# A later landing time for every transfer in the order finder of a two-layer trunk kernel

## The chip, the cores and the metric

The kernel runs on one core of one Trainium2 chip. The metric is device time in microseconds (us) of one execution. A core has five engines that run side by side, each through its own list of instructions in order: PE (TensorE, matmuls), DVE (VectorE), ACT (ScalarE), POOL (GpSimd) and SP (SyncE, which here only issues DMA transfers). An instruction that must wait for another engine or for a transfer holds up everything behind it in its own list.

## The reference

A trunk of two layers on 256 tokens of width 1024, all in float32. Each layer is a gated feed-forward (width 2816), a mixer with two kinds of attention, and a second gated feed-forward; each of the three is wrapped in a normalization whose shift, scale and gate come from a vector `c`:

```python
for l in range(2):
    mod = silu(c) @ ada_w[l] + ada_b[l]          # 1024 x 9216 weights, one row
    sh1, sc1, g1, sh2, sc2, g2, sh3, sc3, g3 = split(mod, 9)
    h = rmsnorm(x, norm_pre[l, 0]) * (1 + sc1) + sh1
    y = (silu(h @ w_gate) * (h @ w_up)) @ w_down
    x = x + 0.5 * g1 * rmsnorm(y, norm_post[l, 0])
    h = rmsnorm(x, norm_pre[l, 1]) * (1 + sc2) + sh2
    y = mixer(h)                                  # 8 sliding-window heads, 8 causal heads
    x = x + g2 * rmsnorm(y, norm_post[l, 1])
    ...                                           # second feed-forward, with sh3, sc3, g3
```

## The kernel before, in words

**Weights.** Every weight block is 1 MiB. SP loads it into a tile `raw` (pool of 3, `NRAW`), and `unit` splits it by quarters into two halves of the precision: ACT writes `hi` (L450), DVE writes `lo` = raw - hi (L451). A `raw` tile is free for the next load when DVE has written the last quarter of its `lo`. PE multiplies three products per block: in the feed-forward's columns L498 and L501 (`mm2t`, 512 and 256 columns), elsewhere L489, L490 and L491 (`mm3`). The feed-forward runs over the hidden width in 11 blocks of 256 columns, `w_gate` and `w_up` by columns (L498, L501; ACT and DVE empty their PSUM tiles `w` in L725 and L726), `w_down` by rows (accumulators `a`).

**Modulation in the background.** The vectors sh, sc, g that are needed later come from `ada_w`, 512 KiB at a time: SP loads a tile `araw` (L534, pool of 2), DVE multiplies and adds it into `acc` in two instructions (L526, "sums" below), and when eight are done ACT and DVE split the sum (L541, L542) and PE adds it up over the partitions (L543, L544, `over_partitions`), after which ACT or DVE (L554, L557, L560) makes the row. A new `araw` can be issued when the sums of the one two before it are done.

**The opening.** The first two vectors (shift and scale of the first normalization) can't wait for that. They are computed by quarters q of 256 columns on PE itself from tiles `eraw` (L937; L1009 for q = 0, L1013 after), then DVE adds the bias row (L1017), PE spreads the row over the partitions (L1018), DVE applies it to both halves of the tokens (L1026, L1027), and `to_T` turns the result (PE L618) into `hT` (ACT L621, DVE L622). As each quarter is ready, PE multiplies it with a quarter of the first weight columns ("first", four accumulators) and of the next ones ("next", L1047 to L1049).

**The order.** The program is written once, and then `keep_order` decides in which order each engine runs its instructions. It knows an estimated duration of each (`cost`) and plays the program forward: an engine takes, among the instructions that it believes ready, the one of the best priority. A transfer ends in its model when a single queue has moved its bytes, and whoever reads it is ready a fixed time later, `READY["SP"]` for ACT, with values of their own for DVE and PE. `forward` runs once from the written priorities and four times (`FBI`) from those that `backward` derives; the shortest result in its own estimate gives the lists, which are then fixed by order edges between neighbours:

```python
gap = AFTER[e] if eng[j] == e and not dma[k] else READY.get((e, eng[j]), READY[e])
ready[j] = max(ready[j], end + gap if preds[j][k] else start)
```

The hardware then obeys the lists: what the finder believed of the times has no further effect than the order.

Of the kernel before, what the change touches and what calls it, by code (L numbers as in the profile page):

```python
# [41 lines left out]

READY = {("SP", "DVE"): 1000, ("SP", "PE"): 1100, "SP": 910, ("PE", "DVE"): 290, "PE": 200, ("DVE", "PE"): 235,
         "DVE": 200, ("Activation", "PE"): 275, "Activation": 145, "Pool": 60}
AFTER = {"SP": 0, "PE": 0, "DVE": 125, "Activation": 100, "Pool": 90}
FBI, BSLACK, FSLACK = 4, {'DVE': 60, 'Activation': 40}, {'DVE': 370, 'Activation': 810}
# [34 lines left out]
def keep_order(tc, nc, slots, shifts):  # L83
# [72 lines left out]
    def forward(prio):  # L156
# [33 lines left out]
        for _ in range(10 * N):  # L190
# [50 lines left out]
            for j in succs[k]:  # L241
                npred[j] -= 1
                gap = AFTER[e] if eng[j] == e and not dma[k] else READY.get((e, eng[j]), READY[e])
                ready[j] = max(ready[j], end + gap if preds[j][k] else start)
# [9 lines left out]
    def backward(at_, reuse):  # L254
# [16 lines left out]
        while True:  # L271
# [8 lines left out]
            for j, kind in ps[k].items():  # L280
                nsucc[j] -= 1
                if kind is True:
                    gap = AFTER[eng[j]] if eng[j] == e and not dma[j] else READY.get((eng[j], e), READY[eng[j]])
                else:
# [830 lines left out]
```

## Time and profile before

| | |
|---|---|
| median of 3 runs | 1038.66 us (1036.26 to 1040.55) |
| profiled execution | 1039.74 us, its span 1038.0 us |
| PE busy | 1004.7 us, 97% of the span |
| DVE busy | 846.6 us, 82% |
| ACT busy | 597.9 us, 58% |
| mean DMA rate | 252 GB/s |

PE is busy nearly throughout, and 33.3 us of its span are idle. So the time can change only where PE waits: by waits that go, or by new ones. The profiled execution lies 1.74 us above its span, which is what lies around the first and last instruction.

### The profile page before, as it was taken

The page shows a single profiled execution, that of the slowest core. Times are in us where ns is not written, and L with a number is a line of the kernel's source. Part 1 is how long each engine was busy: PE and PEld are TensorE (multiplying, and loading weights), DVE is VectorE, ACT ScalarE, POOL GpSimd, SP SyncE. Part 2 cuts the span into 40 slices and gives each one's busy share as a digit, 9 for nine tenths or more (in the row PEclk, how much of TensorE's full clock was granted, in tenths as well). Part 3 has the DMA queues.
Part 4 walks back from the last instruction along what each step waited for, and adds up shares of the span by engine and source line. Part 5 has one row for each costly group of instructions (what it writes and reads, how often), then busy time and mean ns, then how long its engine had stood idle before and what let it go on. Part 6 is the DMA issues. An engine that isn't in the chain of part 4 may idle for free. (4 is left out here: it accounts for less than half of the span.)

```text
span 1038.0 us, 15309 instructions
## 1 busy us (share of the span) xinstructions
PE 1004.7 (97%) x5386; PEld 840.7 (81%) x5386; DVE 846.6 (82%) x1640; ACT 597.9 (58%) x1398; POOL 44.7 (4%) x92
## 2 busy tenths in 40 slices
PE   7999998999999999999999999999999999999997
PEld 4787877788887888888888888888788778888886
DVE  3698998888996898898989988988978789665652
ACT  3365545564676875656756655554577766554541
POOL 1000000001001100000010000000200020000000
PEclk9999999999999999999999999999999999999999
DMA  9999889785997388788757988887589638555521
GB/s 322 340 332 333 271 295 313 261 288 191 315 316 259 94 286 296 239 289 296 255 202 263 308 290 286 316 278 280 174 285 329 207 123 290 182 197 187 182 78 40
DMA packets 171976, 261.82 MB, mean 252 GB/s; under 512 B 6524, under 2 KB 107612, under 8 KB 171900
## 3 DMA queue, kind: packets, MB, share of 16 engines
q1 hardware_dynamic: 171744, 260.78, 74.5%
q8 instruction: 42, 0.69, 0.3%
q14 instruction: 34, 0.28, 0.1%
q10 hardware_dynamic: 156, 0.07, 0.0%
HBM read 259.76 MB, written 1.07 MB: 251 GB/s over the span
## 5 line engine op out<-in xcount | busy, mean ns | idle before, releaser
L451 DVE TENSOR_TENSOR lo_a<-raw_a,hi_a 128x512 fp32r<-128x512 f32 (+1 forms) x548 | 296.3, 586 | 25.9 <-PE w_b L501 8.0
L450 ACT ACTIVATE hi_a<-raw_a 128x512 fp32r<-128x512 f32 (+1 forms) x548 | 262.2, 542 | 78.4 <-DMA raw_a<-in_ffn_w_up_dram 18.7
L498 PE MATMUL w_a<-hT,hi_a 128*128 128x512 f32 x608 | 213.2, 398 | 2.7 <-DVE row_b L557 1.3
L498 PE MATMUL w_b<-hT,hi_b 128*128 128x512 f32 x512 | 180.4, 398 | 2.6 <-DVE st_a L726 1.6
L501 PE MATMUL w_a<-hT,lo_a 128*128 128x256 f32 x608 | 158.5, 281 | 0.0
L450 ACT ACTIVATE hi_b<-raw_b 128x512 fp32r<-128x512 f32 (+1 forms) x224 | 106.5, 544 | 47.7 <-DMA raw_b<-in_ffn_w_up_dram 19.6
L501 PE MATMUL w_b<-hT,lo_b 128*128 128x256 f32 x512 | 133.4, 281 | 0.0
L451 DVE TENSOR_TENSOR lo_b<-raw_b,hi_b 128x512 fp32r<-128x512 f32 (+1 forms) x224 | 122.3, 588 | 12.9 <-PE w_a L501 5.5
L498 PEld LDWEIGHTS w_a<-hT,hi_a 128*128 128x128 f32 x608 | 110.8, 188 | 24.8 <-DVE row_b L557 1.6
L501 PEld LDWEIGHTS w_a<-hT,lo_a 128*128 128x128 f32 x608 | 114.8, 189 | 6.7
L498 PEld LDWEIGHTS w_b<-hT,hi_b 128*128 128x128 f32 x512 | 93.7, 188 | 22.2 <-DVE st_a L726 2.2
L501 PEld LDWEIGHTS w_b<-hT,lo_b 128*128 128x128 f32 x512 | 96.6, 189 | 6.4 <-issue 0.6
L526 DVE SCALAR_TENSOR_TENSOR acc_a<-araw_a,ccol,acc_a 128x512 f32<-128x512 f32 x115 | 85.8, 746 | 9.2 <-DMA araw_a<-in_ada_w_dram 8.1
L490 PE MATMUL a_b<-lo_a,str_a 128*128 128x512 f32 x156 | 60.9, 390 | 0.0
L491 PE MATMUL a_b<-hi_a,str_a 128*128 128x512 f32 x156 | 60.9, 390 | 0.0
L489 PE MATMUL a_b<-hi_a,str_a 128*128 128x512 f32 x156 | 60.4, 391 | 0.0
L725 ACT ACTIVATE st_a<-w_a 128x256 f32<-128x256 f32 x76 | 28.5, 377 | 50.6 <-PE w_a L498 50.1
L725 ACT ACTIVATE st_b<-w_b 128x256 f32<-128x256 f32 x64 | 24.0, 377 | 49.4 <-PE w_b L498 49.4
L726 DVE TENSOR_TENSOR st_a<-w_a,st_a 128x256 f32<-128x256 f32 x76 | 31.7, 419 | 18.2 <-ACT st_a L725 18.0
L597 POOL TENSOR_SCALAR rstd_a<-ss_a 128x1 f32<-128x1 f32 x13 | 6.9, 531 | 725.4 <-ACT junk L647 700.5
L509 PE MATMUL w_a<-hT,hi_a 128*128 128x256 f32 x128 | 37.1, 292 | 0.0
L489 PE MATMUL w_a<-hi_a,hT 128*128 128x512 f32 (+1 forms) x96 | 36.4, 379 | 0.5 <-DVE hT L622 0.5
(262 smaller groups left out, 1978.2 us busy)
## 6 DMA issues: line engine op xcount, KB each, us to landing
araw_a<-in_ada_w_dram SPq DMA_DIRECT2D x86, 512.0 KB
raw_a<-in_ffn_w_down_dram SPq DMA_DIRECT2D x30, 1024.0 KB
raw_a<-in_ffn_w_gate_dram SPq DMA_DIRECT2D x25, 1024.0 KB
raw_a<-in_ffn_w_up_dram SPq DMA_DIRECT2D x25, 1024.0 KB
araw_b<-in_ada_w_dram SPq DMA_DIRECT2D x42, 512.0 KB
raw_a<-in_mix_w_in_dram SPq DMA_DIRECT2D x18, 1024.0 KB
raw_b<-in_ffn_w_gate_dram SPq DMA_DIRECT2D x16, 1024.0 KB
raw_b<-in_ffn_w_up_dram SPq DMA_DIRECT2D x16, 1024.0 KB
```

Source lines behind the costliest of these rows:

```text
L450: nc.scalar.activation(hi[:, sl], raw[:, sl], AF.Copy)
L451: nc.vector.tensor_sub(lo[:, sl], raw[:, sl], hi[:, sl].bitcast(F32))
L489: nc.tensor.matmul(ps_, hh, wh, start=start, stop=False)
L490: nc.tensor.matmul(ps_, hh, wl, start=False, stop=False)
L491: nc.tensor.matmul(ps_, hl, wh, start=False, stop=stop)
L498: both = lambda **f: nc.tensor.matmul(ps_, wh, hTa[:, kt], **f)
L501: nc.tensor.matmul(ps_[:, :256], wl, hT[0][:, kt], start=False, stop=False)
L509: nc.tensor.matmul(ps_, wh, hh, start=start, stop=False)
L526: nc.vector.scalar_tensor_tensor(acc[:, :n], raw[:, t, :], ccol[:, k:k + 1], b if t == 0 else acc[:, :n], op0=ALU.mult, op1=ALU.add)
L597: nc.gpsimd.tensor_scalar(r, s0, 1.0 if s1 is None else s1, EPS, op0=ALU.mult if s1 is None else ALU.add, op1=ALU.add)
L725: nc.scalar.activation(dst, p_[:, 256:], AF.Copy)
L726: nc.vector.tensor_add(dst, p_[:, :256], dst)
```

## The change

All transfers count as landing 2.6 us later in the finder's model: for readers on ACT 3510 ns after the bytes instead of 910, on DVE 3600 instead of 1000, on PE 3700 instead of 1100. No instruction is added or removed; the program on the chip differs by the order alone.

```diff
-READY = {("SP", "DVE"): 1000, ("SP", "PE"): 1100, "SP": 910, ("PE", "DVE"): 290, "PE": 200, ("DVE", "PE"): 235,
+READY = {("SP", "DVE"): 3600, ("SP", "PE"): 3700, "SP": 3510, ("PE", "DVE"): 290, "PE": 200, ("DVE", "PE"): 235,
          "DVE": 200, ("Activation", "PE"): 275, "Activation": 145, "Pool": 60}
```

The lists differ on PE, DVE, ACT and SP, from the first instructions to the sixth section of the program; the end is the same. Three places follow. A number at the end of a name is the tile's; `lo_a_618` belongs to `hi_a_617`, and so on.

**Place one, the opening, SP and DVE.** SP's list (a piece of the difference, + is the changed one) at the loads for the quarters q = 1 and 2; `araw_b_846` and `araw_b_851` are the first background transfers, `eraw` and `raw_a` belong to the opening:

```order
 L945 DMA str_a_314<-in_norm_pre_dram 128x512
+L534 DMA araw_b_846<-in_ada_w_dram 128x2x512
+L532 DMA gb<-in_ada_b_dram 1x512
+L534 DMA araw_b_851<-in_ada_w_dram 128x2x512
+L391 DMA brow_a_1248<-in_norm_post_dram 128x512
+L937 DMA eraw_a_319<-in_ada_w_dram 128x8x256
+L438 DMA raw_a_309<-in_ffn_w_gate_dram 128x2x256
 L937 DMA eraw_a_312<-in_ada_w_dram 128x8x256
-L937 DMA eraw_a_319<-in_ada_w_dram 128x8x256
+L438 DMA raw_a_316<-in_ffn_w_gate_dram 128x2x512
```

Two background transfers and a broadcast row now stand ahead of the opening's loads. DVE's list at quarter q = 1 before (`st_a_344` and `st_b_374` are the two token halves that PE turns next, `lo_a_353` the quarter's first weights):

```order
L1026 SCALAR_TENSOR_TENSOR st_a_344<-w_a_324,str_a_203 128x256
L1027 TENSOR_TENSOR st_a_344<-st_a_344,w_a_324 128x256
L1026 SCALAR_TENSOR_TENSOR st_b_374<-w_a_324,str_b_253 128x256
L1027 TENSOR_TENSOR st_b_374<-st_b_374,w_a_324 128x256
L622 TENSOR_TENSOR hT<-w_a_347,hT 128x2x128
L451 TENSOR_TENSOR lo_a_353<-raw_a_169,hi_a_352 128x512
```

and of the change at the same place:

```order
L1026 SCALAR_TENSOR_TENSOR st_a_344<-w_a_324,str_a_203 128x256
L526 SCALAR_TENSOR_TENSOR acc_b_845<-araw_b_846,ccol,gb 128x512
L1027 TENSOR_TENSOR st_a_344<-st_a_344,w_a_324 128x256
L1026 SCALAR_TENSOR_TENSOR st_b_374<-w_a_324,str_b_253 128x256
L526 SCALAR_TENSOR_TENSOR acc_b_845<-araw_b_846,ccol,acc_b_845 128x512
L1027 TENSOR_TENSOR st_b_374<-st_b_374,w_a_324 128x256
L622 TENSOR_TENSOR hT<-w_a_347,hT 128x2x128
L526 SCALAR_TENSOR_TENSOR acc_b_845<-araw_b_851,ccol,acc_b_845 128x512 x2
L451 TENSOR_TENSOR lo_a_353<-raw_a_169,hi_a_352 128x512 x4
```

The first four background sums have moved in between the steps of the opening's chain and ahead of its weights' `lo`.

**Place two, DVE where the opening ends.** `lo_a_618` is the last "next" block, whose `raw` tile (543) the load of `raw_b_776` takes over; before:

```order
L451 TENSOR_TENSOR lo_a_576<-raw_a_431,hi_a_575 128x512 x4
L622 TENSOR_TENSOR hT<-w_b_600,hT 128x2x128
L526 SCALAR_TENSOR_TENSOR acc_b_845<-araw_b_851,ccol,acc_b_845 128x512 x2
L451 TENSOR_TENSOR lo_a_618<-raw_a_543,hi_a_617 128x256 x4
L451 TENSOR_TENSOR lo_a_692<-raw_a_689,hi_a_691 128x512
```

and of the change, where the first two quarters of `lo_a_618` stand nine rows above these and the last two here:

```order
L451 TENSOR_TENSOR lo_b_728<-raw_b_725,hi_b_727 128x512 x4
L542 TENSOR_TENSOR ast_a_953<-acc_b_845,ast_a_952 128x512
L526 SCALAR_TENSOR_TENSOR acc_b_1129<-araw_b_1130,ccol,gb 128x512
L526 SCALAR_TENSOR_TENSOR acc_b_1129<-araw_b_1130,ccol,acc_b_1129 128x512
L451 TENSOR_TENSOR lo_a_618<-raw_a_543,hi_a_617 128x256
L526 SCALAR_TENSOR_TENSOR acc_b_1129<-araw_b_1135,ccol,acc_b_1129 128x512
L451 TENSOR_TENSOR lo_a_618<-raw_a_543,hi_a_617 128x256
```

The block's `lo` has moved behind the next two blocks' and behind sums of transfers that are issued after it.

**Place three, ACT in the first feed-forward.** `hi_b_1835` is the split of a `w_up` block, `st_a_1618` the emptying of the two PSUM tiles of a `w_gate` block; before:

```order
L541 ACTIVATE ast_a_1674<-acc_b_1568 128x512
L450 ACTIVATE hi_b_1776<-raw_b_1774 128x512 x4
L450 ACTIVATE hi_b_1835<-raw_b_1833 128x512
L725 ACTIVATE st_a_1618<-w_a_1619 128x256
L541 ACTIVATE ast_b_1847<-acc_a_1683 128x512
L725 ACTIVATE st_a_1618<-w_a_1638 128x256
L450 ACTIVATE hi_b_1835<-raw_b_1833 128x512 x3
```

and of the change:

```order
L450 ACTIVATE hi_a_1736<-raw_a_1734 128x512 x4
L661 ACTIVATE str_a_1357<-st_a_1257 128x512
L725 ACTIVATE st_a_1618<-w_a_1619 128x256
L450 ACTIVATE hi_b_1776<-raw_b_1774 128x512 x3
L725 ACTIVATE st_a_1618<-w_a_1638 128x256
L450 ACTIVATE hi_b_1776<-raw_b_1774 128x512
L541 ACTIVATE ast_b_1847<-acc_a_1683 128x512
L450 ACTIVATE hi_b_1835<-raw_b_1833 128x512
```

Both emptyings now stand ahead of the split of the block that is loaded last.

## Rows read from the trace of the kernel before

**Rows 1.** Page, parts 1 and 2: busy us of each engine; clock in tenths:

```profile
PE 1004.7 (97%) x5386; PEld 840.7 (81%) x5386; DVE 846.6 (82%) x1640; ACT 597.9 (58%) x1398; POOL 44.7 (4%) x92
...
PEclk9999999999999999999999999999999999999999
```

**Rows 2.** PE in order of time, 98 to 196 us: start us, us, what [idle before <-releaser]:

```profile
99.91 0.50 PE L498 MATMUL w_a<-hT,hi_a 128*128 128x512 f32 x1 [1.26 <-ACT row_a L554]
...
177.15 0.50 PE L498 MATMUL w_b<-hT,hi_b 128*128 128x512 f32 x1 [1.05 <-DVE st_a L726]
178.17 0.50 PE L498 MATMUL w_b<-hT,hi_b 128*128 128x512 f32 x1 [0.52 <-DVE st_a L726]
179.97 0.50 PE L498 MATMUL w_a<-hT,hi_a 128*128 128x512 f32 x1 [1.31 <-DVE row_b L557]
...
195.64 0.51 PE L543 MATMUL w_b<-ast_b,onesr 128*128 128x512 f32 x1 [2.42 <-DVE st_b L726]
```

**Rows 3.** ACT in order of time, at the same places:

```profile
97.18 2.19 ACT L450 ACTIVATE hi_b<-raw_b 128x512 fp32r<-128x512 f32 x4 [5.90 <-DMA raw_b<-in_ffn_w_up_dram]
99.28 0.58 ACT L554 ACTIVATE row_a<-w_a 128x512 f32<-128x512 f32 x1
...
175.74 0.63 ACT L450 ACTIVATE hi_b<-raw_b 128x512 fp32r<-128x512 f32 x1 [7.22 <-DMA raw_b<-in_ffn_w_up_dram]
176.27 0.37 ACT L725 ACTIVATE st_a<-w_a 128x256 f32<-128x256 f32 x1
...
194.23 0.63 ACT L450 ACTIVATE hi_a<-raw_a 128x512 fp32r<-128x512 f32 x1 [4.13 <-DMA raw_a<-in_ffn_w_up_dram]
194.76 0.37 ACT L725 ACTIVATE st_b<-w_b 128x256 f32<-128x256 f32 x1
```

**Rows 4.** SP (issues of transfers) in order of time:

```profile
59.87 0.37 SPq L438 DMA_DIRECT2D raw_b<-in_ffn_w_up_dram  x1
...
168.20 0.37 SPq L438 DMA_DIRECT2D raw_b<-in_ffn_w_up_dram  x1
...
862.91 0.37 SPq L438 DMA_DIRECT2D raw_b<-in_ffn_w_down_dram  x1
```

**Rows 5.** ACT in order of time, where loaded data are read first:

```profile
14.02 0.63 ACT L627 ACTIVATE junk<-x 128x512 bf16<-128x512 f32 x1 [7.56 <-DMA x<-in_x_dram]
...
65.01 0.63 ACT L450 ACTIVATE hi_b<-raw_b 128x512 fp32r<-128x512 f32 x1 [1.60 <-DMA raw_b<-in_ffn_w_gate_dram]
...
867.91 1.15 ACT L450 ACTIVATE hi_b<-raw_b 128x512 fp32r<-128x512 f32 x2 [0.71 <-DMA raw_b<-in_ffn_w_down_dram]
```

**Rows 6.** Page, part 5: line engine op, out<-in xcount | busy, mean ns | idle before:

```profile
L451 DVE TENSOR_TENSOR lo_a<-raw_a,hi_a 128x512 fp32r<-128x512 f32 (+1 forms) x548 | 296.3, 586 | 25.9 <-PE w_b L501 8.0
```

**Rows 7.** DVE in order of time, in the opening:

```profile
16.59 0.75 DVE L989 SCALAR_TENSOR_TENSOR str_b<-x,rstd_a,str_a 128x512 f32<-128x512 f32 x1 [3.12 <-POOL rstd_a L599]
...
56.97 1.52 DVE L526 SCALAR_TENSOR_TENSOR acc_b<-araw_b,ccol,acc_b 128x512 f32<-128x512 f32 x2
58.41 1.42 DVE L451 TENSOR_TENSOR lo_a<-raw_a,hi_a 128x256 fp32r<-128x256 f32 x4
```

**Rows 8.** PE in order of time, in the opening:

```profile
20.18 0.44 PE L618 MATMUL w_b<-ident,st_b 128*128 128x128 f32 x2 [0.35 <-DVE st_b L1027]
21.74 0.80 PE L489 MATMUL a_a<-hi_a,hT 128*128 128x512 f32 x1 [1.13 <-ACT hT L621]
...
36.60 0.41 PE L618 MATMUL w_b<-ident,st_b 128*128 128x128 f32 x2 [0.34 <-DVE st_b L1027]
...
44.25 1.93 PE L1013 MATMUL w_a<-eraw_a,ccol 128*32 128x256 f32 x32
...
79.16 0.62 PE L498 MATMUL w_b<-hT,hi_b 128*128 128x512 f32 x2
```

**Rows 9.** Busy us of each engine, clock, DMA share, GB/s, by window of time:

```profile
core 0: us, PE busy (x) PEld busy (x) DVE busy (x) ACT busy (x) POOL busy (x), PEclk, DMA share, GB/s
60.00:70.00 10.00, 9.85 (x57) 8.47 (x56) 8.55 (x14) 6.69 (x13) 0.00 (x0) 1.00 1.06 365
```

## The prediction

> **What bounds the kernel now.** I began with the page: PE is busy 1004.7 of 1038.0 us, and the granted clock is in the highest tenth in every slice of the span [rows 1], so the matmuls run at the upper of the two clock levels throughout and nothing is to be had from the clock. What can change is the 33.3 us in which PE is idle. Next I read PE in order of time for the places where it stands still inside the first feed-forward. At 99.91 it waits 1.26 us for a row that ACT makes, at 177.15, 178.17 and 179.97 it waits 1.05, 0.52 and 1.31 us for emptied PSUM tiles and for a row behind them, and at 195.64 it waits 2.42 us [rows 2]. Then I read ACT at those times, to see what held the releaser. It is the same thing each time: ACT stood for 5.90, 7.22 and 4.13 us at the first split of a weight block that had not landed, and right behind that split, in the same list, stood the short instruction that PE wanted: L554 at 99.28, L725 at 176.27 and at 194.76 [rows 3]. The instruction itself is short (0.37 to 0.58 us); what costs is its place behind a late load. So the finder believed that these loads land earlier than they do, and the three places cost 1.26 + 2.88 + 2.42 = 6.56 us of PE.
>
> How late are loads? From SP's issue to the first read I find 862.91 to 867.91, 5.0 us, and 168.20 to 175.74, 7.5 us [rows 4, 5, 3]. The bytes take 1.05 MB / 365 GB/s = 2.9 us at the rate of a full stretch [rows 9], so 2.1 to 4.6 us come on top. The finder reckoned 0.9; now it reckons 3.5, in the middle. By that the new margin is the better estimate where the queue is full.
>
> **The change, part by part.** No instruction is added or removed and the operands are the same, so PE's 1004.7 us stay; the sum consists of waits. I go by places.
>
> *Costs in the opening.* (1) SP's list moves the load of `eraw_a_151` (1 MiB) ahead of the second half of `x`: that half comes 2.9 us later, ACT's square of it goes from 14.02 to about 16.9 [rows 5], DVE's `str_b` from 16.59 to 19.5 [rows 7], and PE's turn of the second token half, at 20.18 [rows 8], to 21 or later. The second product of PE's list now needs that half. PE has only the turns to do up to there, and its products begin at 21.74 [rows 8], 1.6 us behind the turn, so I take +0.4 (0 to 1.2). (2) At quarter q = 1, two background sums stand between the steps of DVE's chain. Two sums in a row take 1.52 us, the pair at 56.97 giving 0.67 to 0.77 each [rows 7], so `st_b` comes 1.4 us later, and PE, which waits for it at 36.60 already [rows 8], waits up to 1.4 longer; it has two products of the quarter ahead of that turn now (some 0.5 us), so +0.9 (0 to 1.4). (3) At q = 3 the last quarter of the weights' `lo` stands behind two more sums: +0.8 (0 to 1.5). The loads of q = 2 and 3 come later too: `eraw_a_321` has 15.25 MiB of list ahead of its end instead of 12.0, 3.41 MB / 365 GB/s = 9.3 us. PE reads it at 44.25 before [rows 8]; its list has moved this read back by 5.1 us of other products, and the load ended well before 44.25 as PE did not wait there. I take 0 (0 to 2).
>
> (4) Where the opening ends. `raw_b_725` has 22.0 MiB ahead of its end in SP's list instead of 19.5: 2.62 MB / 365 = 7.2 us later, so its first read goes from 65.01 [rows 5] to 72.2. DVE then does its four quarters (0.6 us each by the page [rows 6], ACT ahead of them: to 75.0), L542, three sums (0.67 each) and the two last quarters of `lo_a_618` (0.35 each): 75.0 + 0.6 + 2.0 + 0.7 = 78.3. Only then is the tile of block 543 free, and `raw_b_776` can be issued. Before, `lo_a_618` ended at 59.83 [rows 7], and SP issued the load at 59.87 [rows 4]: the same rule, 18 us earlier. With 5.0 to 7.5 us the load can be split at 83.3 to 85.8, and PE has its first halves 0.55 + 0.6 us later, at 84.5 to 87.0. PE wanted this block at 79.4 (the second of the pair at 79.16 [rows 8]); in the changed list 1.9 us more of other products stand ahead, and (1) to (3) have made it 2.1 late: 83.4. So a new wait of 1.1 to 3.6 us, taken as +2.0; its bounds are 0.5 and 4.
>
> The opening then costs 0.4 + 0.9 + 0.8 + 2.0 = +4.1 (0.5 to 10). Behind it, DVE has done 20 sums by the end of the block's `lo` instead of 9: 11 x 0.67 = 7.3 us of work brought forward, on an engine that is busy 8.55 of 10 us there [rows 9]. That is work that DVE hasn't to do later, so I count it at nothing beyond (4); what covers it is the 1.45 us in 10 that DVE is free.
>
> *Gains behind the opening.* In the changed lists the instructions that PE wanted stand ahead of the late splits at the three places (the third place of the change shows one of them: both L725 ahead of `hi_b_1835`). Of the 140 L725, 61 stand behind fewer bytes of loads than before, 62 behind as many, 17 behind more. So I take two thirds of the 6.56 us: −4.4. The bounds are 0, if other instructions are caught behind other late splits instead, and −9, if smaller waits of the same kind go too.
>
> *Sum.* The profiled execution took 1039.74 us, 1.74 of it around the span, and lies 1.08 above the median of 1038.66. 1039.74 + 4.1 − 4.4 = 1039.4, which by the median is 1038.4; I forecast **1038.5**. With the bounds of the two terms it lies between 1033 and 1044.
>
> **A rule weighed.** The two issues show a lateness of 2.1 to 4.6 us over the bytes, that is, one that varies [rows 3 to 5]. The Trainium skill, DMA: Bandwidth & Descriptors, section "Anatomy of one DMA — SWDGE (gpsimd) path", states a fixed part of about 2.0 us for one transfer, beside bytes over 436 GB/s. By it a 1 MiB load would take an estimated 4.4 us, the trace shows 5.0 as its shortest, and all beyond that would be waiting for one's turn and not a constant of a transfer; a margin of the same size on all would then not be what cures a late load.
>
> **The rivals.** (a) *Slower: the opening's end starves.* `raw_b_776` waits not only for three sums but for the load that the last of them reads, `araw_b_1135`, which itself can be issued only when the tile of two before it is summed, about 72. With 5.0 to 7.5 us it is there at 77 to 79.5, `lo_a_618` ends at 78.0 to 80.5, and PE's wait becomes up to 5.8 us. From there the rest follows: DVE is 7.3 us behind on an engine with 1.45 us in 10 to spare, so the stalls of the next three or four blocks don't heal, and the gain of place three is not had. It decides if PE's wait for this block is over 5 us. 1038.66 + 2.1 + 5.8, less 0 to 4.4: 1042 to 1046.6, say 1045. For it: the fence of place two. Against: the wait is bounded by the products that stand ahead. (b) *The margin cures nothing.* The lateness is that of the turn in the queue (the 7.22 us of wait [rows 3] fell on a load issued only 7.5 us before), and a later issue makes it late again: the gain is 0, the opening's cost stays, 1038.66 + 4.1 = 1043. (c) *Faster.* All of the 6.56 us go and a part of the smaller waits with them, and the opening hides its costs, since the new list of PE holds other products of a quarter ahead of each read that comes late: 1038.66 − 6.56 − 0.5 = 1031.5. For it: each place of rows 2 has the same cause. Against: PE waited at 36.60 already. (d) *Nothing comes of it*: the changed lists hold the same number of caught instructions and the opening's costs are hidden: 1038.7.
>
> **How the numbers follow.** Forecast 42%, (a) 15%, (b) 13%, (c) 18%, (d) 12%. About 0.5%, 5.2 us, is what a measurement can tell here: 1033.5 to 1043.9. Faster: all but a sixth of (c), and of the forecast's own spread about a tenth: 0.20. Slower: three quarters of (a), four tenths of (b), and a tenth of the forecast: 0.21. Within: 0.59. The forecast's own range is 1033 to 1044; for 8 in 10 it must hold (c) in most of its width and (a) in most: 1030.5 to 1047.
>
> **What would show it.** In the changed profile: PE idle 1 to 4 us at about 83 us ahead of the first L498 on the first `w_up` block, with that block's issue on SP right behind the last quarter of `lo_a_618` at about 78; more idle time of PE at 36 to 39; no idle place like those at 177 to 180 and 195.6; ACT's waits for `w_up` loads with nothing behind them that PE wants. The prediction is wrong if PE's idle time before 100 us does not grow, if the same evacuations are still caught, or if PE's idle sum leaves 28 to 39 us.

## The result and the profile after

The changed kernel takes 1023.0 us (median of 4 runs, 1022.33 to 1023.22), the kernel before 1038.71 in the same comparison: ratio 0.9849, 95% interval 0.9828 to 0.9870. I had forecast 1038.5, in a range from 1030.5 to 1047. The change is faster by 15.7 us, and the range was missed by 7.5. One execution of e18 below took 1908.5 us in a slower state of the chip and is left out of the figures.

The span went from 1038.0 to 1021.4 us. Page of the changed kernel, part 1:

```profile
PE 1000.1 (98%) x5386; PEld 839.4 (82%) x5386; DVE 848.5 (83%) x1640; ACT 600.3 (59%) x1398; POOL 45.2 (4%) x92
```

PE's idle time fell from 33.3 [rows 1] to 1021.4 - 1000.1 = 21.3 us. These 12.0 us are not the whole of the 16.6: PE's busy time fell too, by 4.6 us (1004.7 to 1000.1), for the same 5386 matmuls. What PE still waits for, longest in total first (waits of PE: engine, line, releaser, us in total, times, longest):

```profile
PE a_b L981 <- DVE mhalf L381: 3.6, 1, 3.6
PE w_a L756 <- DVE st_a L803: 2.2, 2, 1.4
PE a_a L490 <- DVE lo_a L451: 1.9, 2, 1.3
PE w_a L618 <- DVE st_a L1027: 1.3, 2, 1.0
PE w_b L618 <- DVE st_b L1027: 1.1, 1, 1.1
```

Not one of the waits of the feed-forward (L498 or L543 behind L726, L554 or L557, [rows 2]) is left. From 98 us to the last L498 of the first feed-forward, a stretch in which PE of before was idle for 7.4 us, it is busy throughout (window of the changed kernel: length, busy us of PE, PEld, DVE, ACT and POOL, clock, DMA share, GB/s):

```profile
98.00:211.14 113.14, 113.14 (x596) 96.16 (x595) 109.03 (x186) 68.27 (x139) 0.00 (x0) 1.00 0.94 316
```

That is 0.19 us for each of 596 matmuls, while an L498 lasts 0.40 us and an L501 0.28 in the page's mean: in an unbroken stream they overlap. Beside a wait they don't: the three L498 of [rows 2] at 177.15 to 179.97 stand alone with 0.50 us each. So a wait costs more than the idle time that is noted for it, and when it goes, some busy time goes with it.

The weight blocks don't go out earlier, on the whole, than PE's work does: the 25th load of one is issued 12.5 us later than before, the 37th 2.8 and the 61st 12.6 us earlier, where PE is about 1 us behind, 1 and 13 us ahead. (Loads of the background do, the 25th at 144.7 instead of 155.3 us; but in e1, a kernel below that gains more, it goes out at 158.5.) ACT still waits for the blocks. What changed is what stands behind the wait. ACT of the changed kernel in order of time, to set against [rows 3]:

```profile
170.67 1.68 ACT L450 ACTIVATE hi_b<-raw_b 128x512 fp32r<-128x512 f32 x3 [1.91 <-DMA raw_b<-in_ffn_w_gate_dram]
172.25 0.36 ACT L725 ACTIVATE st_a<-w_a 128x256 f32<-128x256 f32 x1
...
174.36 0.63 ACT L450 ACTIVATE hi_b<-raw_b 128x512 fp32r<-128x512 f32 x1 [0.71 <-DMA raw_b<-in_ffn_w_up_dram]
174.90 0.37 ACT L725 ACTIVATE st_a<-w_a 128x256 f32<-128x256 f32 x1
```

ACT waits 1.91 and 0.71 us there instead of 7.22. Over the whole span, the waits of ACT's splits for their blocks sum to 94.5 us before and 54.6 after, those of DVE's background sums (L526) for their tiles to 33.3 and 5.3. In return ACT waits longer for PE in front of its emptyings (L725), which now stand ahead: 99.5 us in 70 waits before, 136.6 us in 107 after.

Where along the span the time was won shows in two instructions of PE: the last L498 of the first feed-forward and the first of the next. Before:

```profile
218.31 0.40 PE L498 MATMUL w_a<-hT,hi_a 128*128 128x512 f32 x1
...
374.83 0.48 PE L498 MATMUL w_a<-hT,hi_a 128*128 128x512 f32 x1
```

and after:

```profile
211.14 0.40 PE L498 MATMUL w_a<-hT,hi_a 128*128 128x512 f32 x1
...
361.86 0.47 PE L498 MATMUL w_a<-hT,hi_a 128*128 128x512 f32 x1
```

So 7.2 us come from the opening and the first feed-forward together, 13.0 - 7.2 = 5.8 from the first layer's mixer, and the last 16.6 - 13.0 = 3.6 from all that follows. The 7.2 are a loss and a larger gain. Towards the end of the opening there is a point by which each kernel has started the same 349 matmuls, by line and tile (PE alone: length of the window, busy us, clock, DMA share, GB/s; before, after, and e1, which is explained below):

```profile
0.00:67.90 67.90, 61.48 (x349) 0.95 1.01 331
0.00:71.30 71.30, 62.64 (x349) 0.98 0.98 325
0.00:64.41 64.41, 58.97 (x349) 1.00 1.00 330
```

The change is 3.4 us behind there, and gains 3.4 + 7.2 = 10.6 us from there to the end of the first feed-forward: 7.9 of idle and 2.7 of busy time.

In the opening the clock did something that I had overlooked. Windows of before (columns as in the window from 98 us):

```profile
20.00:25.00 5.00, 3.69 (x10) 2.78 (x11) 3.12 (x9) 2.69 (x8) 0.00 (x0) 0.59 1.10 349
25.00:30.00 5.00, 5.00 (x18) 4.00 (x17) 0.39 (x2) 0.00 (x0) 0.00 (x0) 0.73 1.07 374
```

and after:

```profile
20.00:25.00 5.00, 3.69 (x11) 2.59 (x12) 4.40 (x9) 3.88 (x10) 0.00 (x0) 0.70 1.07 370
25.00:30.00 5.00, 5.00 (x31) 3.81 (x34) 1.52 (x5) 0.79 (x3) 0.00 (x0) 0.96 1.07 373
```

The granted clock is at the lower of the two levels (1.2 GHz) for part of these ten microseconds: the mean of 0.59 and 0.73 is 0.34 below full, that is 6.8 us at half speed before, 3.4 after. That is worth 1.7 us of PE's time, and the waits of the opening took more than that back.

### The profile page after: what moved, and what is told of

It reads as the page before. It is cut to its first block, busy times and chain, and to the rows that moved or that the text cites. A ratio compares the mean times of both kernels' runs of the same rounds, so it can differ in the third digit from the quotient of the medians.

```text
span 1021.4 us, 15319 instructions
## 1 busy us (share of the span) xinstructions
PE 1000.1 (98%) x5386; PEld 839.4 (82%) x5386; DVE 848.5 (83%) x1640; ACT 600.3 (59%) x1398; POOL 45.2 (4%) x92
## 5 line engine op out<-in xcount | busy, mean ns | idle before, releaser
L498 PE MATMUL w_a<-hT,hi_a 128*128 128x512 f32 x608 | 212.2, 397 | 0.0
L498 PE MATMUL w_b<-hT,hi_b 128*128 128x512 f32 x512 | 179.4, 397 | 0.0
L501 PE MATMUL w_a<-hT,lo_a 128*128 128x256 f32 x608 | 158.3, 281 | 0.0
L501 PE MATMUL w_b<-hT,lo_b 128*128 128x256 f32 x512 | 132.9, 281 | 0.0
L498 PEld LDWEIGHTS w_a<-hT,hi_a 128*128 128x128 f32 x608 | 110.6, 188 | 21.3
L501 PEld LDWEIGHTS w_a<-hT,lo_a 128*128 128x128 f32 x608 | 114.7, 189 | 7.0
L498 PEld LDWEIGHTS w_b<-hT,hi_b 128*128 128x128 f32 x512 | 93.4, 188 | 18.6 <-ACT bq L416 0.6
L501 PEld LDWEIGHTS w_b<-hT,lo_b 128*128 128x128 f32 x512 | 96.5, 189 | 6.1
L526 DVE SCALAR_TENSOR_TENSOR acc_a<-araw_a,ccol,acc_a 128x512 f32<-128x512 f32 x115 | 86.0, 748 | 4.1 <-DMA araw_a<-in_ada_w_dram 2.5
L725 ACT ACTIVATE st_a<-w_a 128x256 f32<-128x256 f32 x76 | 29.1, 382 | 71.3 <-PE w_a L498 70.7
L725 ACT ACTIVATE st_b<-w_b 128x256 f32<-128x256 f32 x64 | 24.0, 383 | 65.9 <-PE w_b L498 65.9
L726 DVE TENSOR_TENSOR st_a<-w_a,st_a 128x256 f32<-128x256 f32 x76 | 31.9, 421 | 15.6 <-ACT st_a L725 15.4
```

The lines of the kernel that those rows point to most:

```text
L498: both = lambda **f: nc.tensor.matmul(ps_, wh, hTa[:, kt], **f)
L501: nc.tensor.matmul(ps_[:, :256], wl, hT[0][:, kt], start=False, stop=False)
L526: nc.vector.scalar_tensor_tensor(acc[:, :n], raw[:, t, :], ccol[:, k:k + 1], b if t == 0 else acc[:, :n], op0=ALU.mult, op1=ALU.add)
L725: nc.scalar.activation(dst, p_[:, 256:], AF.Copy)
L726: nc.vector.tensor_add(dst, p_[:, :256], dst)
```

## The experiments

All but e3 and e5 change only the finder's numbers, or where they count. Three theories: A, readers: later landing makes the finder put short instructions that PE wants ahead of work that waits for a transfer. B, loads: it makes transfers go out earlier. C, scatter: any new draw of the lists moves the time. The ratio is to the kernel before on the same chip, with its 95% interval; "ACT" and "DVE" are the waits of ACT's splits and of DVE's sums for transfers in us, summed from the view of waits of one profiled execution.

| kernel | believed 2.6 us later | us | ratio | ACT | DVE |
|---|---|---|---|---|---|
| before | nothing | 1038.7 | 1 | 94.5 | 33.3 |
| after | all | 1023.0 | 0.985 | 54.6 | 5.3 |
| e1 | all, forward play only | 1017.2 | 0.977 (0.974 to 0.981) | 49.6 | 1.3 |
| e2 | all, due times only | 1054.4 | 1.013 (1.009 to 1.018) | 119.3 | 31.5 |
| e6 | readers on ACT | 1039.7 | 1.000 (0.998 to 1.003) | 44.3 | 42.1 |
| e7 | readers on DVE | 1032.5 | 0.991 (0.988 to 0.995) | 131.2 | 3.1 |
| e15 | background's tiles | 1039.7 | 0.999 (0.998 to 1.001) | 128.4 | 4.6 |
| e16 | all but the background's | 1039.3 | 0.999 (0.997 to 1.001) | 30.1 | 38.8 |
| e9 | all that end after 75 us | 1022.7 | 0.982 (0.976 to 0.989) | 45.7 | 2.2 |
| e10 | all that end until 75 us | 1041.8 | 1.001 (0.997 to 1.005) | 90.0 | 36.5 |

(e6, e7, e9, e10, e15 and e16 in the forward play only.)

**The two passes apart (e1, e2).** The finder uses the landing time twice: in the forward play for when a reader is ready, and in the backward pass for due times. e1 leaves the due times as they were:

```diff
-                    gap = AFTER[eng[j]] if eng[j] == e and not dma[j] else READY.get((eng[j], e), READY[eng[j]])
+                    gap = AFTER[eng[j]] if eng[j] == e and not dma[j] else READYB.get((eng[j], e), READYB[eng[j]])
```

with `READYB` the values of before. e2 is the reverse. 

> The margin of 2.6 us counts only where the finder plays the program forward (when a reader of a transfer is ready); the passes that derive the due times keep the old values. Theory A (readers: what counts is that short instructions which PE wants are put ahead of splits of late blocks) expects most of the 15.7 us: 1023 to 1028 us. Theory B (loads: what counts is that due times make transfers go out earlier) expects little: 1035 to 1040. Theory C (scatter: any new draw of the lists moves the time by some per cent, up or down) expects no relation, anything from 1020 to 1045.

> The margin counts only in the passes that derive the due times; when a reader is ready keeps the old values. Theory A (readers) expects 1034 to 1040 us, with PE idle again behind short ACT instructions caught behind late splits. Theory B (loads) expects 1023 to 1028. Theory C (scatter) expects anything from 1020 to 1045.

Theory A is right on the half that acts: the forward play alone gives 0.977, more than the change and 6 us below A's own range. The due times alone cost 1.3%, which no theory had named: 1054.4 us lies above all three ranges. B falls.

**The caught instructions alone (e3, e5).** The narrowest form of A is my prediction's own mechanism. e3 keeps every list of before but ACT's, and there moves an instruction fed by PE ahead of a late split:

```diff
-    order = best[0]
+    order = repair(best, eng, dma, preds, users, taken)
```

whose core is

```
for q in range(max(0, p - 6), p) if fed and at_[x][0] > 75000 else ():
    ...
    if not load or max(at_[j][1] for j in load) + 3510 < max(at_[j][1] for j in fed) + 200:
        continue
    o.insert(q, o.pop(p))
    if sound():
        break
```

> The lists of PE, DVE, POOL and SP are those of the kernel before, instruction by instruction. In ACT's list alone, from 75 us of the finder's clock on, an instruction that reads a PE result is moved ahead of a split up to six places before it, where the split's block would land later than the PE result with 2.6 us more. Theory A in its narrow form (the caught instructions on ACT are the loss) expects PE's idle places at 177 to 180 us (2.88) and 195.6 (2.42) to go and a few smaller ones of the later sections: 5 to 9 us, 1030 to 1034. Theory B (loads) and the view that all lists must change together expect 1037 to 1040.

It gave 1.0013 (0.9982 to 1.0044): nothing. DVE and PE of e3 at the place of [rows 2]:

```profile
177.29 0.75 DVE L526 SCALAR_TENSOR_TENSOR acc_b<-araw_b,ccol,gb 128x512 f32<-128x512 f32 x1 [0.58 <-DMA araw_b<-in_ada_w_dram]
177.96 0.42 DVE L726 TENSOR_TENSOR st_a<-w_a,st_a 128x256 f32<-128x256 f32 x1
```

```profile
99.99 0.80 PE L498 MATMUL w_a<-hT,hi_a 128*128 128x512 f32 x1 [3.12 <-ACT row_a L554]
...
178.44 0.49 PE L498 MATMUL w_b<-hT,hi_b 128*128 128x512 f32 x1 [1.17 <-DVE st_a L726]
```

ACT's emptying now ends early (173.74 plus 0.38), but the second half of the pair, L726 on DVE, stands behind a background sum that waits for its own transfer. And the wait at 99.91 grew from 1.26 to 3.12. So e5 repairs DVE's list too. 

> PE, POOL and SP run the lists of the kernel before. In ACT's and in DVE's list, from 75 us of the finder's clock on, an instruction fed by PE (on DVE by ACT too) is moved ahead of a split or a background sum up to six places before it, where that one's transfer would land later with 2.6 us more. In the run with ACT's list alone repaired, PE still waited 1.17 and 1.78 us at 178.4 and 195.3, each time for an L726 on DVE behind a background sum or a split. Theory A2 (caught on ACT and on DVE, and that is the whole loss) expects these idle places to go and 1027 to 1033 us. Theory D (the loss is not the place of single instructions: the order in which PE and SP run has to change with them) expects less than 4 us: 1036 to 1043.

1.0105 (1.0074 to 1.0136): slower. In PE's list of e5 the wait at 182.44 is 3.25 us, for L557 on DVE, which stands behind a sum that waited 1.40 for its transfer and two quarters of `lo`. Moving instructions one by one in lists made for other times moves the waits; theory D of that expectation is right that this repair doesn't gain, though the time lies 8 us above D's range too. What isn't tested is which list carries the gain: no run gives PE or SP alone the order of the change.

**Which readers, which transfers (e6, e7, e15, e16).** The values of one reader in `READY`, or one class of transfers: e15 adds

```diff
+ RD = READYL if dma[k] and any(slots.get(x.bass_ap.tensor.name, "  ")[0].startswith("araw") for x in L[k].outs if getattr(x, "bass_ap", None) is not None) else READY
```

> The 2.6 us count in the forward play only, and only for readers on ACT. If the believed time of ACT's splits is the term, 1017 to 1024 us; if DVE's readers (sums and lo) are the term, 1036 to 1043; if both are needed, in between, about 1030.

> The 2.6 us count in the forward play only, and only for readers on DVE (the background sums, and lo where it reads a tile). If DVE's readers are the term, 1017 to 1024 us; if ACT's splits are, 1036 to 1043; if both are needed, about 1030.

> 2.6 us in the forward play, only for the background's transfers (the 512 KiB tiles araw). If the background's sums on DVE, believed ready too early, are what holds up the instructions that PE wants, most of the 23 us: 1017 to 1025. If the weight blocks are, 1036 to 1043. If both are needed together, 1028 to 1035.

> 2.6 us in the forward play, for all transfers but the background's. If the weight blocks are the term, 1017 to 1025; if the background's sums are, 1036 to 1043; if both are needed together, 1028 to 1035.

Each half alone gives nothing or a little (0.991 for e7), both give 0.977. The last two columns of the table go with that: what is believed late is waited for less, and what isn't is waited for more, and PE's idle time stays (31.1 us in e6, 32.6 in e15 and 31.5 in e16, against 33.3 before; 28.0 in e7). With the background's tiles alone late (e15) the sums' waits fall to 4.6, and the splits' rise to 128.4; with all but them (e16) it is the other way round. The rows that PE then waits behind, first e15 (ACT, then PE),

```profile
171.13 0.63 ACT L450 ACTIVATE hi_b<-raw_b 128x512 fp32r<-128x512 f32 x1 [10.57 <-DMA raw_b<-in_ffn_w_gate_dram]
171.67 0.61 ACT L541 ACTIVATE ast_a<-acc_b 128x512 fp32r<-128x512 f32 x1
```

```profile
172.33 0.50 PE L543 MATMUL w_a<-ast_a,onesr 128*128 128x512 f32 x1 [3.12 <-ACT ast_a L541]
```

and e16 (DVE, then PE):

```profile
187.90 0.75 DVE L526 SCALAR_TENSOR_TENSOR acc_b<-araw_b,ccol,acc_b 128x512 f32<-128x512 f32 x1 [1.88 <-DMA araw_b<-in_ada_w_dram]
188.57 0.42 DVE L726 TENSOR_TENSOR st_b<-w_b,st_b 128x256 f32<-128x256 f32 x1
```

```profile
189.04 0.50 PE L543 MATMUL w_b<-ast_b,onesr 128*128 128x512 f32 x1 [1.82 <-DVE st_b L726]
```

A short instruction is caught behind a split in the one and behind a sum in the other.

**Scatter and size (e4, e8, e11, e12).** e4 is the change with 50 ns in place of 2600; the other three are e1 with 1300, 2700 and 5200.

> A margin of 50 ns instead of 2600: the lists change in many places, but nothing is believed to be later in a way that counts. Theories A and B expect the time of before within 3 us: 1036 to 1042. Theory C (scatter) expects it to be off by 5 us or more, up or down.

> 1.3 us instead of 2.6, in the forward play only, for all readers. If the gain follows the margin, about half of the 23 us: 1026 to 1031. If the margin acts as a threshold that has to cover the lateness over the bytes of at least 2.1 us, little: 1034 to 1041. Theory C (scatter) expects no relation.

> A neighbour of the margin of 2.6 us: 2.7 us in the forward play, for all readers. If the margin itself is what acts, the time is that of its neighbour within 5 us: 1012 to 1022. By theory C (scatter) it may lie anywhere between 1020 and 1045.

> Twice the margin, 5.2 us in the forward play. The longest time from issue to first read that I had found was 7.5 us, the mean in the first feed-forward of before 7.1 us, against 2.9 us for the bytes, so a margin of 5.2 us is above the mean lateness. If the margin has to match the real lateness, this gives part of the gain back: 1018 to 1028. If later is always better (only the direction counts), 1005 to 1015.

e4: 0.9946 (0.9921 to 0.9970), 6 us below the kernel before in the same comparison. That is what theory C had expected of this run, and A and B not: a new draw of the lists alone can be worth half a per cent, and a difference of that size can't be told from one. e8: 0.9885 (0.9842 to 0.9928), half the gain for half the margin. e11: 0.9781 (0.9724 to 0.9837), as its neighbour. e12: 1.0068 (1.0038 to 1.0098), and not faster though ACT's splits wait only 20.2 us and DVE's sums not at all; PE's idle time is 40.4 us. A good part of the price stands in one row of PE:

```profile
221.05 0.79 PE L543 MATMUL w_a<-ast_a,onesr 128*128 128x512 f32 x1 [11.10 <-ACT ast_a L541]
```

ACT's L541 waited for the last background sums (2.48 us of its own idle time, for L526). The sums, believed late, were put off until PE had nothing else, and in those 11.1 us the granted clock fell to the lower level too and stayed there after PE went on (windows of e12):

```profile
215.00:220.00 5.00, 0.00 (x0) 0.00 (x0) 4.93 (x8) 2.19 (x4) 0.00 (x0) 0.50 0.99 348
220.00:225.00 5.00, 3.95 (x11) 3.33 (x12) 4.79 (x8) 2.82 (x5) 0.00 (x0) 0.50 1.04 389
```

Theory C alone doesn't explain the result: the gain is four times that of e4, and the four values 50, 1300, 2600 and 2700 give 0.995, 0.989, 0.977 and 0.978, in order of size up to the last pair, whose intervals overlap nearly whole. With 5200 the order ends.

**By stage (e9, e10, e13, e14).** The margin counts only for transfers that end, by the finder's clock, in one stretch (`end > 75000`, and so on).

> 2.6 us in the forward play only, and only for transfers that the finder sees end after 75 us; the lists of the opening are those of before. My prediction said that the change costs 4.1 us in the opening: then this gains more than the margin over the whole program (1017.2), about 1013. If the opening gives part of the gain (the granted clock did not fall there when the margin counted for the whole forward play), 1020 to 1027. Theory C (scatter): no relation.

> 2.6 us in the forward play only, and only for transfers that the finder sees end before 75 us; from about 75 us on the lists are nearly those of before. By the prediction's opening term this is slower than before by 1 to 4 us: 1040 to 1043. If the opening gains (earlier start of PE's products, no stretch at the lower clock), 1033 to 1037.

> 2.6 us in the forward play, only for transfers that the finder sees end between 75 and 200 us of its clock, that is, in the first feed-forward. The run with all transfers after 75 us had its last L498 of the first feed-forward 7.9 us earlier than before. If the first feed-forward gains by its own transfers and keeps what it gains, about 7 to 9 us: 1030 to 1033. If the gain is lost again in the mixer, 1037 to 1041.

> 2.6 us in the forward play, only for transfers that the finder sees end after 200 us. With all transfers after 75 us, the part behind the first feed-forward gained 17.5 - 7.9 = 9.6 us. If the later stages gain by their own transfers, 1029 to 1033; if they only inherited from the first feed-forward, 1037 to 1041.

The opening alone: 1.001 over the whole program, though in its profile PE ended the 519th matmul at 97.28 us, 5.0 earlier than before (102.27); the stages behind it lost that again. All behind the opening: 0.982. The first feed-forward alone: 0.9960 (0.9927 to 0.9994), no more than e4's scatter, although in its profile the last L498 of that stage came at 208.24, 10.1 us earlier than before; by the first L498 of the next feed-forward (370.93) 3.9 were left. (This profile is of the slowest of ten executions, and about 3.4 of the 6.2 us lost in between fit its two stretches at the lower clock, mean 0.83 from 285 to 295 and from 310 to 320 us.) Everything behind 200 us: 0.9900 (0.9867 to 0.9933). So the later stages gain by their own transfers; that they give back what the stage before them won, if their lists are made with the old values, is what the profiles of e10 and e13 suggest, one execution each.

**The due times (e17, e18).** e1 with other values in `READYB`: 0.8 us less than before, and 1.3 us more.

> 2.6 us in the forward play; in the passes that derive the due times 0.8 us less than before (110 ns for ACT, 200 for DVE, 300 for PE). If later due times cost in a regular way (0.8% for 2.6 us), 0.8 us less gain a quarter of that: 1014 to 1016. If each value just draws another list, no relation to the 1017 of the value 0: 1012 to 1027, up or down.

> 2.6 us in the forward play, 1.3 us in the passes that derive the due times. If the due times cost in a regular way, half way between 1017 and 1023: 1019 to 1021. If each value just draws another list, anywhere from 1012 to 1027.

1018.1 (0.9820, 0.9798 to 0.9842) and 1020.6 (0.9846, 0.9825 to 0.9868). In the order of the due times' margin, -0.8, 0, 1.3 and 2.6: 1018.1, 1017.2, 1020.6, 1023.0 us, or by ratio 0.982, 0.977, 0.985 and 0.985. From 0 on the times rise, and less than 0 gains nothing; with a scatter of half a per cent, that later due times cost in a regular way is not shown. Where the change loses against e1 the windows at 349 matmuls show: it is 71.30 - 64.41 = 6.9 us behind e1 there, and 6.5 at the end of the span. So the due times of the change cost in the opening. Why e2 is slower than before stays open; in its profile PE is idle for 40.6 us and the mean granted clock is 0.990, against 33.3 and 0.995 before. e1, 1017.2 us, has the lowest time of the study; e17 and e11 lie within 1.1 us of it.

## Why the prediction was wrong, point by point

**The failed step is the gain behind the opening**, "two thirds of the 6.56 us: −4.4". Behind the opening the change won 10.6 + 5.8 + 3.6 = 20.0 us, far outside my lower bound of −9 for the term. In the first feed-forward all 6.56 us at the three places went, 1.3 of smaller idle time and 2.7 of busy time, which "PE's 1004.7 us stay" had fixed; 5.8 us in the first mixer and 3.6 behind it came from places that I hadn't priced at all. I had listed only those idle places of PE where ACT's row showed a late weight block just ahead, all of them in the first feed-forward. The background's sums on DVE wait for transfers as well, and the view of waits had this: 33.3 us in before, beside 94.5 of the splits. One such place in the mixer of before (DVE, ACT, PE):

```profile
292.04 0.75 DVE L526 SCALAR_TENSOR_TENSOR acc_a<-araw_a,ccol,gb 128x512 f32<-128x512 f32 x1 [1.50 <-DMA araw_a<-in_ada_w_dram]
292.71 0.28 DVE L842 CUSTOM_DVE_ANT_0 st_a<-w_a,bias_a 128x128 f32<-128x128 f32 x1
293.03 0.40 ACT L847 ACTIVATE st_a<-st_a,negm_a 128x128 f32<-128x128 f32 x1 [1.70 <-DVE negm_a L842]
293.58 0.33 PE L853 MATMUL w_a<-ident,st_a 128*128 128x128 f32 x1 [1.04 <-ACT st_a L847]
```

A sum stood 1.50 us for its tile; behind it, in DVE's list, stood a step of the attention (L842) that ACT (L847) and then PE (L853) wanted. e16 shows that with the sums left out nothing is gained.

**The mechanism** (short instructions caught behind late transfers) was right in kind: e1 against e2, and the rows of e15 and e16. That it can be counted and cured place by place was wrong: e3 and e5 move the caught instructions in lists that stay as they are otherwise, other waits take their place, and nothing is gained.

**The bounds.** Those of my two terms, 0.5 to 10 and 0 to −9, add up to 1030.2 to 1048.7 us about the median, not to the 1033 to 1044 that I wrote; the measured time lies outside both. Of the signs of being wrong that I had named, one came: PE's idle sum, 21.3 us, left 28 to 39.

**The opening, +4.1.** (1) The second token half's turn came at 21.54 with 1.14 us of waiting (predicted 21 or later), but PE's products began at 21.74 as before: 0 instead of +0.4. And the clock, of which I had written that nothing is to be had, gave 1.7 us. PE of the changed kernel:

```profile
21.54 0.44 PE L618 MATMUL w_b<-ident,st_b 128*128 128x128 f32 x2 [1.14 <-DVE st_b L1027]
21.74 0.55 PE L489 MATMUL a_a<-hi_a,hT 128*128 128x512 f32 x1
...
36.30 0.73 PE L489 MATMUL a_a<-hi_a,hT 128*128 128x512 f32 x2 [0.47 <-ACT hT L621]
...
63.67 0.50 PE L490 MATMUL a_a<-lo_a,hT 128*128 128x512 f32 x1 [1.31 <-DVE lo_a L451]
66.53 0.50 PE L490 MATMUL a_a<-lo_a,hT 128*128 128x512 f32 x1 [0.59 <-DVE lo_a L451]
...
82.65 0.40 PE L498 MATMUL w_b<-hT,hi_b 128*128 128x512 f32 x1
```

(2) At q = 1, 0.47 and 0.29 us of waits instead of 0.34 [rows 8], +0.4 against +0.9. (3) The `lo` behind the sums cost 1.31 + 0.59 = 1.9 against +0.8, the one term that was too small. (4) The wait at the opening's end, +2.0, didn't come: PE's first L498 on the `w_up` block, at 82.65, has no idle time ahead of it. I had taken it that `raw_b_776` needs the tile of block 543, as in the lists before. But SP issued it right when DVE had ended the `lo` of block 689 (73.29 + 1.29 = 74.58); SP and ACT of the changed kernel:

```profile
74.60 0.37 SPq L438 DMA_DIRECT2D raw_b<-in_ffn_w_up_dram  x1
```

```profile
81.75 2.20 ACT L450 ACTIVATE hi_b<-raw_b 128x512 fp32r<-128x512 f32 x4
```

That is 3.7 us before the 78.3 that I had worked out, and 7.2 us from issue to read (ACT stood at an emptying for PE just before, so the block may have landed earlier); PE came to it at 82.65 (predicted 83.4). Which tile a load takes in this kernel follows the order in which tiles come free, and the change had altered this order as well.

The sum came out near +4.1, at 3.4 us by the 349th matmul, but by luck: (4) was nothing, (3) more than twice its size, the clock gave 1.7 back, and 62.64 - 61.48 + 1.7 = 2.9 us are busy time of PE, which I had held fixed; why the same matmuls took longer there is not shown beyond the missing overlap beside the waits. e10 doesn't test this sum: its opening is made with the due times of before, and the 349 matmuls are started by 65.35 us, 2.6 earlier than in the kernel before.

**The rivals.** (a) needed the wait at the opening's end and fell with it. (b), that a fixed margin cures nothing since the lateness varies, was refuted by 15.7 us: it need not match each load, being near the middle of 2.1 to 4.6 us was enough, and with twice the margin nothing was gained (e12). The rule that I had weighed is from the Trainium skill, DMA: Bandwidth & Descriptors, section "Anatomy of one DMA — SWDGE (gpsimd) path": a fixed part of about 2.0 us per transfer, fitted for transfers issued from GpSimd, while SP issues the loads here. It is close to the shorter of the two latenesses that I had read, 2.1 us. But lateness believed to be 0.91 + 1.3 = 2.2 us (e8) gave half of the gain that 3.5 us (e1) gave. (c), "all of the 6.56 us go and a part of the smaller waits with them", had the right mechanism, 1031.5 us and a chance of 18%; it too counted single places. (d), that nothing comes of it, is 15.7 us off.

## What to carry to other kernels

Where a planner fixes in-order lists, an estimate that is too early costs more than the wait itself: everything queued behind the waiting instruction waits too, on each engine that reads transfers, and here only lists planned together, with all transfers believed later, were rid of it. Read the lateness from the trace (issue to first read, less the bytes), put it where the plan decides who is ready, and try half and double of it. And before pricing a gain from a few idle places, sum the waits by releaser over all engines: 94.5 and 33.3 us stood in the profile of before. Such sums show where to look and not what there is to gain: e12 has the smallest, and it isn't faster. What counts is the idle time of the engine that is busy nearly throughout, and the overlap that it loses beside each wait.

## What the runs showed of the hardware

In the kernel before a stretch of 6.8 us at the lower clock began at about 21 us, after pauses of PE of 1.03 and 0.35 us ahead of its instructions at 19.39 and 20.18 us and within a third, of 1.13 us ahead of 21.74; it is hidden in a page whose slices are 26 us long. In e1, where PE's products began at 20.22, the mean of the clock from 20 to 30 us is 1.00. The chip's spread for one and the same kernel was larger than expected: medians of the kernel before lay between 1037.6 and 1042.1 us in the six comparisons, where four executions of the changed kernel lay within 0.9 us. The spread goes with the clock: of the 86 executions of the kernel before in the comparisons of e1 to e18, the four that took 1050 us and more had a mean granted clock of 0.989 to 0.992 and the fastest, 1034.2 us, 0.998, and a straight line through all 86 falls by 1.0 us for 0.001 of the clock. Since the clock falls upon pauses, that doesn't part its cost from theirs.
